# One 512-column product with the weights' hi half for both halves of the operand, in 23 chunks, and the gate bias in two tiles

## The chip, the cores and the metric

The kernel runs on one core of a Trainium2 chip. The metric is the time of one execution on the device in microseconds (us); lower is better. The time before the change is 834.99 us, the median of three runs (832.32 to 836.01).

The core has TensorE (PE; its weight loads are told apart as PEld), VectorE (DVE), ScalarE (ACT) and GpSimd (POOL), which run their own queues in order, and SyncE (SP), whose queue issues the loads from memory here. PE writes to PSUM only, and DVE and ACT take the results from there.

## What is computed

Two blocks of a network over 256 positions of width 1024, in 32-bit floating point. Cut to what the change touches:

```
# first block
h = rmsnorm(x, mix_pre_norm)
u = h @ w_in                       # split into u_z, u_xbc, u_dt, u_ly, u_lx, u_g
y_a = ssd_mixer(u_z, u_xbc, u_dt)  # ends with a norm of y * silu(u_z)
y_b = rglru_mixer(u_ly, u_lx)      # u_lx goes through a causal convolution of 4 taps, two gate products, a scan
g = sigmoid(u_g + gate_b)
x = x + rmsnorm((g0 * (y_a @ w_proj_ssm) + g1 * (y_b @ w_proj_lru)) @ w_out)
x = x + rmsnorm(ffn(rmsnorm(x)))
# second block
cols = rmsnorm(x) @ w_in_2         # split into four branches' inputs (among them xm_q, sw_q, sw_k, sw_v, gm_uv), their z, gate_logits
y_a .. y_m = deltanet, spatial gating, sliding window, memory attention   # each times silu(z)
x = x + rmsnorm(sum_n(sigmoid(gate_logits_n) * (y_n @ w_up_n)) @ w_out_2)
```

## The kernel before

Every weight matrix streams in once, in 129 chunks of two halves (128 x 1024 values each). Of each half ACT makes `whi`, a rounded copy in the fast 32-bit format of PE, and DVE makes `wlo`, the rest (lines 112 and 113). Activations are kept in the same way as `HH` (hi) and `HL` (lo). A product is then three matmuls, hi by hi, hi by lo and lo by hi (`mm3`, lines 425 to 427).

There are two layouts. In `proj_fm` the weights are stationary (128 x 128 blocks) and the activations stream past them, 256 columns (the positions) at a time: one chunk gives 256 output features, in two groups j of 128, each over eight blocks k, so 2 x 8 x 3 = 48 matmuls of 256 columns. In `proj_tm` the activations are stationary and the weights stream, 512 columns at a time, 24 matmuls a chunk.

`Weights` holds three raw halves and five split halves at a time. A load waits until a raw tile is free (its `wlo` done), a split waits until PE has read the tile that it overwrites. All loads stand in SP's queue in order.

PE's order is the order of the code: `Weave` runs the main line (the projections), and at each `yield`, a tick, lets one side line (two in the second block) issue its few instructions. So the matmuls of the recurrent mixers stand between the matmuls of the projections, a fixed number of ticks after what they need was asked for. If that isn't ready, PE waits there. The order on DVE, ACT and SP is set by the framework's scheduler, by when it expects inputs to be ready.

The names that matter below. First block: chunks `ly` (4), `xbc` (6), `z` (4), `lx` (4), `g` (8, layout tm, gate logits, four groups i of two chunks), `pa`, `pb`, `o`. The `z` result is copied from PSUM to `SZ` by one ACT copy of 512 columns a chunk (line 981). The `lx` result goes from PSUM into `conv` (lines 580 to 588: an ACT operation and three DVE operations for each of the two groups, giving `XC`). In the same stretch `side_ssd` runs: for each of 16 heads a PE product `pe`, three ACT exponentials and a DVE product give `M` (line 705), and two ticks later `py` (line 715) reads two `M`. Then `side_lru`: eight products `pg` (line 765) of `XC` with `lw`. The gate bias `gb`, 128 x 2048, is loaded into the buffer of `lw` (lines 990 to 992), so it waits for the last `pg`; DVE adds it to the gate logits of `g` (line 1003). PSUM has four banks (`pp`) for the projections, used in turn.

Second block: `dn` (6 chunks), `xq` (2), `sq` (2), `skv` (1), `gv` (2, tm), `gu` (2), `z2` (8), then `g2` and `up`. Results of `xq`, `sq`, `skv` and `z2` are copied by ACT, 512 columns at a time; `gu` goes through a Gelu from PSUM. They feed the memory branch (`pxs`), the window branch (`psv`, `psc`), and the branches' z.

Of the kernel before, what the change touches and what calls it, by code (L numbers as in the profile page):

```python
# [8 lines left out]
F32 = mybir.dt.float32  # L9
# [187 lines left out]
def two_blocks_kernel(  # L197
# [231 lines left out]
    def proj_fm(name, xh, xl, kouter=False):  # L429
# [19 lines left out]
                    yield  # L449
        return ps, v2(b)  # L450

    def proj_tm(name, xk, nchunk, done, halve=False, before=None):

        w2 = (512, S if halve else 512)
        ps = [[(c0, pbank(f"{name}_{tt}{c0}")) for c0 in range(0, 512, w2[tt])]
              for tt in range(2)]  # L460
        for c in range(nchunk):
            if before:
                yield from before(c)
            wh, wl = W.next(4)
            for tt in range(2):
                t = slice(tt * P, (tt + 1) * P)
                for c0, b in ps[tt]:
                    q = slice(c0, c0 + w2[tt])
                    for k in range(4):
                        h, l = xk(4 * c + k)  # L470
                        mm3(b[:, 0 : w2[tt]], h[:, t], l[:, t], wh[k][:, q], wl[k][:, q],
                            c == 0 and k == 0, c == nchunk - 1 and k == 3)
# [116 lines left out]
                    in1=o[:, d:S], op0=ALU.mult, op1=ALU.add)  # L589


    HH = act8("HH", "HH1", F32R)
    HL = act8("HL", "HL1", F32R)
    wv = Weave(1)

    HU = act8("b3", "HU", F32R)
# [347 lines left out]
            wv.event(f"{nm}{tt}")  # L944
        return then

    def block1(HH, HL):

        late = []
        for p in range(4):  # L950
# [26 lines left out]
            yield  # L977
        SZ = ya["sz"] = act8("b2", "SZ")
        for p in range(4):
            _, b = yield from proj_fm(f"z{p}", HH, HL)  # L980
            nc.scalar.copy(SZ[:, 2 * p : 2 * p + 2, :], b)
            yield
        wv.event("z")
        for p in range(4):
            ps, _ = yield from proj_fm(f"lx{p}", HH, HL)
            two = (2 * p, 2 * p + 1)
            conv([XC[:, i, :] for i in two], ps, "lru_conv_w", two, 8, 4, "lru_conv_b")
            wv.event(f"lx{p}")
            if p == 3:
                gb = big.tile([P, 2 * D], F32, tag="lw", name="gb")  # L990
                with tc.issue_after(W.loaded.ins):
                    nc.sync.dma_start(gb, gbias)
            yield

        G = [big.tile([P, 2, D], F32, tag=("b1", "b9")[n], name=f"G{n}") for n in range(2)]
        for i in range(4):
            n, c = divmod(i, 2)
            q = slice(512 * c, 512 * c + 512)

            def gate(tt, _, ps):  # L1000

                g = G[n][:, tt, q]
                nc.vector.tensor_tensor(out=g, in0=ps, in1=gb[:, 512 * i : 512 * i + 512],  # L1003
                                        op=ALU.add)
                if i == 3:
                    nc.scalar.activation(g, g, AF.Sigmoid)

            yield from proj_tm(f"g{i}", lambda k: (HH[:, k, :], HL[:, k, :]), 2, gate)
            if i == 2:
                nc.scalar.activation(G[0], G[0], AF.Sigmoid)  # L1010
                nc.scalar.activation(G[1][:, :, 0:512], G[1][:, :, 0:512], AF.Sigmoid)
# [23 lines left out]
        yield from M.join(0)  # L1035

        O = []
        HH = act8("HH", "HH2", F32R)
        HL = act8("HL", "HL2", F32R)
        wv.add("n2", side_next("n2", O, HH, HL, "ffn_pre_norm"))  # L1040
        yield from M.out("o", 0, residual("n2", O))

# [26 lines left out]
            yield  # L1069

        O = []
        HH = act8("HH", "HH3", F32R)
        HL = act8("HL", "HL3", F32R)
        wv.add("n3", side_next("n3", O, HH, HL, "norm_pre_2"))
        yield from out_proj("fd", lambda k: (FH[k // 8][:, k % 8, :], FL[k // 8][:, k % 8, :]),
                            6, 1, residual("n3", O), last)
# [2 lines left out]
        yield from proj_tm("mv", lambda k: (em["h"][:, k, :], em["l"][:, k, :]), 2,  # L1079
                           lambda tt, _, ps: nc.scalar.copy(MV[:, tt, :], ps))  # L1080
        yield "n3"
        yield from block2(HH, HL, MK, MV)


    def bc4(ap):
# [4 lines left out]

        return ap.unsqueeze(1).to_broadcast([P, 4, P])

    def block2(HH, HL, MK, MV):
        lws = big.tile([P, 16, P], F32, tag="b8", name="lws")
        wst = lws[:, 0:4, :]
        lvs = lws[:, 4:9, :].rearrange("p a c -> p (a c)")
# [520 lines left out]
                wv.event(f"dn{a}{p}")  # L1617
                yield
        for p in range(2):
            _, b = yield from proj_fm(f"xq{p}", HH, HL)  # L1620
            nc.scalar.copy(XQ[:, 2 * p : 2 * p + 2, :], b)
            if p == 1:
                wv.event("xq")
            yield
        for p in range(2):
            _, b = yield from proj_fm(f"sq{p}", HH, HL)
            nc.scalar.copy(SQ[:, 2 * p : 2 * p + 2, :], b)
            yield
        _, b = yield from proj_fm("skv", HH, HL)
        nc.scalar.copy(SKV, b)  # L1630
        wv.event("skv")
        yield
        yield from proj_tm(
# [1 line left out]
            lambda tt, _, ps: nc.scalar.activation(GV[:, tt, :], ps, AF.Gelu_apprx_tanh))  # L1635
        wv.event("gv")
        for p in range(2):
            _, b = yield from proj_fm(f"gu{p}", HH, HL)
            nc.scalar.activation(GU[:, 2 * p : 2 * p + 2, :], b, AF.Gelu_apprx_tanh)
            if p == 1:  # L1640
                wv.event("gu")
            yield
        for n in (3, 2, 1, 0):
            if n == 0:
                yield "spatial"
            for p in range(2):
                _, b = yield from proj_fm(f"z2{n}{p}", HH, HL)
                nc.scalar.copy(Z[n][:, 2 * p : 2 * p + 2, :], b)
                if p == 1:
                    wv.event(f"z{n}")  # L1650
                yield
# [3 lines left out]
        for n in order:  # L1655
            if n == 0:
                wv.add("y0", branch0())
            G2 = big.tile([P, 2, D], F32, tag="b1", name=f"G2{n}")
            for c in range(2):
                yield from proj_tm(  # L1660
                    f"g2{n}{c}", lambda k: (HH[:, k, :], HL[:, k, :]), 2,
                    lambda tt, _, ps: nc.scalar.activation(
                        G2[:, tt, 512 * c : 512 * c + 512], ps, AF.Sigmoid))
            if n == 3:
                yield "decay"
                yield "delta"
# [12 lines left out]
            if n == order[-1]:  # L1679
                M = Merged(MG, act8("HH", "MH2", F32R), act8("HL", "ML2", F32R), "m2")  # L1680
            for c in range(2):
                q = slice(512 * c, 512 * c + 512)

                def done(tt, _, ps):
                    g, m = G2[:, tt, q], MG[:, tt, q]
                    if n == order[0]:
                        nc.vector.tensor_tensor(out=m, in0=ps, in1=g, op=ALU.mult)
                        return
                    t = tmp(f"mg2{n}{c}{tt}")
                    nc.vector.tensor_tensor(out=t, in0=ps, in1=g, op=ALU.mult)  # L1690
                    nc.vector.tensor_tensor(out=m, in0=m, in1=t, op=ALU.add)
                    if n == order[-1]:
# [19 lines left out]
    def program():  # L1712
        with tc.manual_schedule(engines={nc.scalar.engine, nc.vector.engine}):
            constants()
            for g in range(2):
                for k, _ in enumerate(W.split_pieces(4)):
                    feature(4 * g + k, XT, HU, LU)
                more_loads(g)
            W.split(4)
            for tt in range(2):  # L1720
                nc.scalar.activation(NRM[:, 0:1024], X[:, tt, :], AF.Square,
                                     accum_out=rx[:, tt : tt + 1])
            nc.scalar.activation(rx, rx, AF.Sqrt, bias=eps1, scale=1.0 / D)
            nc.vector.reciprocal(rx, rx)
            dtab.append(small_w(0, 16, "wdt"))
            baab.append(small_w(16, 8, "wba"))
            nc.scalar.activation(ea, row("ssm_a_log"), AF.Exp)
            nc.scalar.activation(ea2, row("a_log_2"), AF.Exp)
            nc.vector.tensor_scalar(nlam, pc[:, lamc : lamc + 8], -1.0, None, op0=ALU.mult)
        yield from block1(HH, HL)  # L1730

    with tc.manual_schedule(engines={nc.tensor.engine}):
        wv.add("rms", side_rms())
# [15 lines left out]
def _layout(inp):  # L1749
# [19 lines left out]
        np.broadcast_to(a(n)[0][None, :], (P, D))  # L1769
        for n in ("mix_post_norm", "ffn_post_norm", "norm_post_2")])  # L1770

    d["gbias"] = np.broadcast_to(a("gate_b")[0].reshape(1, 2 * D), (P, 2 * D))

    parts = []
    for name, n in COLS:
# [94 lines left out]
```

## Time and profile before

| | |
|---|---|
| median of three runs | 834.99 us (832.32 to 836.01) |
| the profiled execution, its own time | 833.6 us |
| its span, first to last instruction | 831.9 us |
| mean granted clock of PE | 0.998 |
| PE busy | 813.5 us, 98% |
| DVE busy | 599.3 us, 72% |
| ACT busy | 519.9 us, 62% |
| POOL busy | 61.1 us, 7% |

The page's times are those of one profiled execution. An operation's duration runs from its start to its end; operations on one engine overlap, so the distance between the starts of two is what one more costs in a row of such. A group's line gives count, busy time and mean duration, then the idle time of the engine just ahead of it and what ended that.

### The profile page before, as it was taken

To read this page: it belongs to the slowest core of one execution; us is meant where nothing else is said; L and a number is where in the kernel's file an instruction comes from. 1 tells how busy PE (TensorE), PEld (TensorE's weight loads), DVE (VectorE), ACT (ScalarE), POOL (GpSimd) and SP (SyncE) were. 2 spreads that over 40 slices of the span, in tenths; PEclk is the share of its full clock that TensorE was granted. 3 is DMA by queue.
4 is the path that set the end of the run, shared out by engine and by line. 5 is a ranking of instruction groups with operands and counts; after the bars stand their busy time and mean duration, and the time that the engine had idled before them with its cause. 6 is when DMAs were issued, how large, how long until landed. Compare 5 with 4: busy or idle time off the path is not lost.

```text
span 831.9 us, 13970 instructions
## 1 busy us (share of the span) xinstructions
PE 813.5 (98%) x5428; PEld 741.5 (89%) x5428; DVE 599.3 (72%) x980; ACT 519.9 (62%) x791; POOL 61.1 (7%) x101
## 2 busy tenths in 40 slices
PE   6999999999999999999999999999999999999997
PEld 6999989778889999999988989998999988888886
DVE  5889678778688788888845597866775547466573
ACT  6575887895656755656644468945966555544452
POOL 0000000000030000000000100028830000000000
PEclk9999999999999999999999999999999999999999
DMA  8546444456754655555655644543554335556551
GB/s 307 194 161 230 142 139 150 169 211 199 250 180 147 218 197 181 176 196 177 209 198 182 196 160 154 199 135 104 164 150 156 121 133 177 194 190 199 190 190 50
DMA packets 41105, 147.15 MB, mean 177 GB/s; under 512 B 4880, under 2 KB 5136, under 8 KB 40784
## 3 DMA queue, kind: packets, MB, share of 16 engines
q1 hardware_dynamic: 40320, 145.35, 51.3%
q0 software_dynamic: 576, 0.92, 0.5%
q8 instruction: 42, 0.69, 0.4%
q14 instruction: 23, 0.19, 0.1%
q10 hardware_dynamic: 144, 0.00, 0.0%
HBM read 144.94 MB, written 1.31 MB: 176 GB/s over the span
## 4 chain that ended last, share of the span: by engine, by line
PE 92%; DVE 4%; DMA 2%; ACT 1%; issue 0%; DVEq 0%; SPq 0%; ACTq 0%
PE fu L427 6%; PE fu L426 6%; PE fu L425 6%; PE g L425 5%; PE g L427 5%; PE g L426 5%; PE z L425 3%; PE z L426 3%; PE z L427 3%; PE fd L426 3%; PE fd L425 3%; PE fd L427 3%; PE up L427 2%; PE up L425 2%; PE up L426 2%; PE o L427 2%
## 5 line engine op out<-in xcount | busy, mean ns | idle before, releaser
L113 DVE TENSOR_TENSOR wlo<-wraw,whi 128x1024 fp32r<-128x1024 f32 x256 | 312.5, 1228 | 145.8 <-ACT whi L112 144.6
L112 ACT CAST whi<-wraw 128x1024 fp32r<-128x1024 f32 x256 | 266.6, 1049 | 219.2 <-PE fu L426 47.5
L425 PE MATMUL fu<-HH,whi 128*128 128x256 f32 x384 | 108.7, 283 | 0.0
L426 PE MATMUL fu<-HL,whi 128*128 128x256 f32 x384 | 108.7, 283 | 0.0
L427 PE MATMUL fu<-HH,wlo 128*128 128x256 f32 x384 | 108.7, 283 | 0.0
L425 PE MATMUL g<-whi,HH 128*128 128x512 f32 x192 | 76.8, 400 | 3.0 <-DVE G L1003 3.0
L427 PE MATMUL g<-whi,HL 128*128 128x512 f32 x192 | 74.9, 390 | 0.0
L426 PE MATMUL g<-wlo,HH 128*128 128x512 f32 x192 | 74.8, 390 | 0.0
L425 PEld LDWEIGHTS fu<-HH,whi 128*128 128x128 f32 x384 | 73.7, 192 | 0.0
L426 PEld LDWEIGHTS fu<-HL,whi 128*128 128x128 f32 x384 | 73.7, 192 | 0.0
L427 PEld LDWEIGHTS fu<-HH,wlo 128*128 128x128 f32 x384 | 73.7, 192 | 0.0
L425 PE MATMUL z<-HH,whi 128*128 128x256 f32 x192 | 56.6, 295 | 0.0
L426 PE MATMUL z<-HL,whi 128*128 128x256 f32 x192 | 54.2, 282 | 0.0
L427 PE MATMUL z<-HH,wlo 128*128 128x256 f32 x192 | 54.2, 282 | 0.0
L425 PEld LDWEIGHTS g<-whi,HH 128*128 128x128 f32 x192 | 36.1, 188 | 10.6 <-DVE G L1003 3.5
L587 DVE SCALAR_TENSOR_TENSOR fc<-fu,pc,fc 128x255 f32<-128x255 f32 (+1 forms) x96 | 43.8, 478 | 1.6
L427 PEld LDWEIGHTS g<-whi,HL 128*128 128x128 f32 x192 | 36.0, 188 | 7.8
L426 PEld LDWEIGHTS g<-wlo,HH 128*128 128x128 f32 x192 | 36.1, 188 | 7.2
L426 PE MATMUL fd<-wlo,FH 128*128 128x512 f32 (+1 forms) x120 | 41.7, 347 | 0.0
L425 PE MATMUL fd<-whi,FH 128*128 128x512 f32 (+1 forms) x120 | 41.6, 347 | 0.0
L427 PE MATMUL fd<-whi,FL 128*128 128x512 f32 (+1 forms) x120 | 41.6, 347 | 0.0
L425 PEld LDWEIGHTS z<-HH,whi 128*128 128x128 f32 x192 | 36.6, 190 | 1.3 <-issue 0.9
(535 smaller groups left out, 2044.1 us busy)
## 6 DMA issues: line engine op xcount, KB each, us to landing
wraw<-in_w_in_dram SPq DMA_DIRECT2D x130, 512.0 KB, 4.0
wraw<-in_w_fu_dram SPq DMA_DIRECT2D x48, 512.0 KB, 4.2
wraw<-in_w_fd_dram SPq DMA_DIRECT2D x24, 512.0 KB, 3.9
wraw<-in_w_o_dram SPq DMA_DIRECT2D x16, 512.0 KB, 4.1
wraw<-in_w_up_dram SPq DMA_DIRECT2D x16, 512.0 KB, 3.6
wraw<-in_w_pa_dram SPq DMA_DIRECT2D x8, 512.0 KB, 3.5
wraw<-in_w_pb_dram SPq DMA_DIRECT2D x8, 512.0 KB, 4.1
wraw<-in_w_mk_dram SPq DMA_DIRECT2D x4, 512.0 KB, 4.2
```

The source lines that it names most:

```text
L112: nc.scalar.copy(hi, raw)
L113: nc.vector.tensor_tensor(out=lo, in0=raw, in1=hi.bitcast(F32), op=ALU.subtract)
L425: nc.tensor.matmul(o, wh, xh, start=first, stop=False)
L426: nc.tensor.matmul(o, wh, xl, start=False, stop=False)
L427: nc.tensor.matmul(o, wl, xh, start=False, stop=last)
L587: nc.vector.scalar_tensor_tensor(o[:, d:S], in0=p[:, 0 : S - d], scalar=col(wname, (taps - 1 - d) * n + i), in1=o[:, d:S], op0=ALU.mult, o ...
```

## The change

In 23 chunks (`z` 4, `lx` 4, `xq` 2, `sq` 2, `skv` 1, `gu` 2, `z2` 8) `proj_fm` gives way to `proj_wide`. HH and HL become one tile `HX`, hi and lo of a block side by side, and `whi` streams both as one product of 512 columns into a whole PSUM bank: hi by hi in columns 0 to 255, hi by lo in 256 to 511. `wlo` by hi goes on top of columns 0 to 255. Each group j has its own bank. Then ACT copies the right half to the result's place and DVE adds the left half to it. For `lx` the result is a new tile `lx_s`, which the convolution reads instead of PSUM; for `gu` the Gelu then runs in place. The other chunks of `proj_fm` and all of `proj_tm` read the same `HX` through views, with the same products as before.

The gate bias is two tiles of 128 x 1024: `gb0` in the buffer `wrow`, which has no earlier user, and `gb1` in that of `lw`.

```
+    def hilo(name):
+        t = big.tile([P, NT, 2, S], F32R, tag="HX", name=name)
+        return t[:, :, 0, :], t[:, :, 1, :], t
...
+    def proj_wide(name, hx, o=None):
+        wh, wl = W.next()
+        ps = [pbank(f"{name}_{j}") for j in range(2)]
+        o = v2(tmp(f"{name}_s")) if o is None else o
+        for j in range(2):
+            f = slice(j * P, (j + 1) * P)
+            for k in range(8):
+                a = (ps[j][:, 0:S], wl[k][:, f], hx[:, k, 0, :])
+                b = (ps[j], wh[k][:, f], hx[:, k].rearrange("p a t -> p (a t)"))
+                for i, p in enumerate((b, a) if k == 0 else (a, b)):
+                    nc.tensor.matmul(*p, start=k + i == 0, stop=k == 7 and i == 1)
+                if k % 4 == 3 and j + k < 8:
+                    yield
+            nc.scalar.copy(o[:, j, :], ps[j][:, S : 2 * S])
+            nc.vector.tensor_tensor(out=o[:, j, :], in0=ps[j][:, 0:S], in1=o[:, j, :], op=ALU.add)
+        return [o[:, j, :] for j in range(2)]
...
-    HH = act8("HH", "HH1", F32R)
-    HL = act8("HL", "HL1", F32R)
+    HH, HL, HX = hilo("HX1")
...
-            _, b = yield from proj_fm(f"z{p}", HH, HL)
-            nc.scalar.copy(SZ[:, 2 * p : 2 * p + 2, :], b)
+            yield from proj_wide(f"z{p}", HX, SZ[:, 2 * p : 2 * p + 2, :])
...
-            ps, _ = yield from proj_fm(f"lx{p}", HH, HL)
+            ps = yield from proj_wide(f"lx{p}", HX)
...
-                gb = big.tile([P, 2 * D], F32, tag="lw", name="gb")
+                gb = [big.tile([P, D], F32, tag=("wrow", "lw")[n], name=f"gb{n}")
+                      for n in range(2)]
                 with tc.issue_after(W.loaded.ins):
-                    nc.sync.dma_start(gb, gbias)
+                    for n in range(2):
+                        nc.sync.dma_start(gb[n], gbias[n])
...
-                nc.vector.tensor_tensor(out=g, in0=ps, in1=gb[:, 512 * i : 512 * i + 512],
-                                        op=ALU.add)
+                nc.vector.tensor_tensor(out=g, in0=ps, in1=gb[n][:, q], op=ALU.add)
...
-        _, b = yield from proj_fm("skv", HH, HL)
-        nc.scalar.copy(SKV, b)
+        yield from proj_wide("skv", HX, SKV)
...
-            _, b = yield from proj_fm(f"gu{p}", HH, HL)
-            nc.scalar.activation(GU[:, 2 * p : 2 * p + 2, :], b, AF.Gelu_apprx_tanh)
+            g = GU[:, 2 * p : 2 * p + 2, :]
+            yield from proj_wide(f"gu{p}", HX, g)
+            nc.scalar.activation(g, g, AF.Gelu_apprx_tanh)
```

What stands where in the queues, at three places. PE, at the start of the chunk `z0`, before:

```order
L425 MATMUL z0_1019<-HH1_103,whi20_832 128x256
L426 MATMUL z0_1019<-HL1_104,whi20_832 128x256
L427 MATMUL z0_1019<-HH1_103,wlo20_833 128x256
L425 MATMUL z0_1019<-HH1_103,whi20_832 128x256
L426 MATMUL z0_1019<-HL1_104,whi20_832 128x256
L427 MATMUL z0_1019<-HH1_103,wlo20_833 128x256
```

and after:

```order
L468 MATMUL z0_0_1018<-HX1_103,whi20_831 128x512
L468 MATMUL z0_0_1018<-HX1_103,wlo20_832 128x256 x2
L468 MATMUL z0_0_1018<-HX1_103,whi20_831 128x512
L468 MATMUL z0_0_1018<-HX1_103,wlo20_832 128x256
L468 MATMUL z0_0_1018<-HX1_103,whi20_831 128x512
```

The first six rows are two blocks k of three products; in the second fence two blocks are the first three rows (four products).

SP's queue, around the load of the gate bias (`wraw` 39 to 49 are raw halves of weights, in the order of use), before:

```order
L87 DMA wraw40_1685<-in_w_in_dram 128x1024
L87 DMA wraw41_1764<-in_w_in_dram 128x1024
L87 DMA wraw42_1770<-in_w_in_dram 128x1024
L87 DMA wraw47_1940<-in_w_in_dram 128x1024
L87 DMA wraw48_1946<-in_w_in_dram 128x1024
L992 DMA gb_1758<-in_gbias_dram 128x2048
L87 DMA wraw49_2024<-in_w_in_dram 128x1024
```

and after:

```order
L87 DMA wraw40_1606<-in_w_in_dram 128x1024
L1015 DMA gb0_1669<-in_gbias_dram 128x1024
L87 DMA wraw41_1677<-in_w_in_dram 128x1024
L87 DMA wraw42_1683<-in_w_in_dram 128x1024
L87 DMA wraw48_1859<-in_w_in_dram 128x1024
L1015 DMA gb1_1670<-in_gbias_dram 128x1024
L87 DMA wraw49_1937<-in_w_in_dram 128x1024
```

The first half of the bias now stands eight weight loads further ahead, between `wraw40` and `wraw41`; the second half stands where the whole stood.

DVE, in the stretch of `lx`, around the product `M13` that `py6` reads (`M13` to `M15` are heads 13 to 15, `lx0_s` is the sum of the chunk `lx0`), before:

```order
L113 TENSOR_TENSOR wlo33_1503<-wraw33_1387,whi33_1502 128x1024
L587 SCALAR_TENSOR_TENSOR XC_123<-lx0_1399,pc_79,XC_123 128x255
L719 SCALAR_TENSOR_TENSOR XS_121<-XS_121,pc_79,py5_1494 128x256
L587 SCALAR_TENSOR_TENSOR XC_123<-lx0_1399,pc_79,XC_123 128x254
L705 TENSOR_TENSOR M13_1489<-M13_1489,bBC_120 128x384
```

and after:

```order
L472 TENSOR_TENSOR lx0_s_1352<-lx0_0_1350,lx0_s_1352 128x256
L727 TENSOR_TENSOR M12_1404<-M12_1404,bBC_119 128x384
L472 TENSOR_TENSOR lx0_s_1352<-lx0_1_1351,lx0_s_1352 128x256
L610 SCALAR_TENSOR_TENSOR XC_122<-lx0_s_1352,pc_79,XC_122 128x255
L741 SCALAR_TENSOR_TENSOR XS_120<-XS_120,pc_79,py5_1435 128x256
L610 SCALAR_TENSOR_TENSOR XC_122<-lx0_s_1352,pc_79,XC_122 128x254
L610 SCALAR_TENSOR_TENSOR XC_122<-lx0_s_1352,pc_79,XC_122 128x255
L610 SCALAR_TENSOR_TENSOR XC_122<-lx0_s_1352,pc_79,XC_122 128x253
L610 SCALAR_TENSOR_TENSOR XC_122<-lx0_s_1352,pc_79,XC_122 128x254
L727 TENSOR_TENSOR M13_1430<-M13_1430,bBC_119 128x384
```

Two additions are new, and `M13` now stands behind five of the six convolution steps of `lx0` instead of two; the split `wlo33` has moved behind it.

## Rows read from the trace of the kernel before

**Rows 1.** The page's first part: busy us (share of the span) x instructions.

```profile
PE 813.5 (98%) x5428; PEld 741.5 (89%) x5428; DVE 599.3 (72%) x980; ACT 519.9 (62%) x791; POOL 61.1 (7%) x101
```

**Rows 2.** The page's chain that ended last: share of the span by engine.

```profile
PE 92%; DVE 4%; DMA 2%; ACT 1%; issue 0%; DVEq 0%; SPq 0%; ACTq 0%
```

**Rows 3.** PE's waits: us in total, times, longest us (the two largest).

```profile
PE ly L425 <- ACT HU L605: 7.0, 1, 7.0
PE g L425 <- DVE G L1003: 3.0, 1, 3.0
```

**Rows 4.** Timeline of PE in a chunk of z: start us, us, instruction.

```profile
83.97 0.28 PE L426 MATMUL z<-HL,whi 128*128 128x256 f32 x1
...
84.69 0.28 PE L426 MATMUL z<-HL,whi 128*128 128x256 f32 x1
```

**Rows 5.** Timeline of PE in a chunk of pa.

```profile
199.74 0.39 PE L426 MATMUL pa<-wlo,YAH 128*128 128x512 f32 x1
199.97 0.39 PE L427 MATMUL pa<-whi,YAL 128*128 128x512 f32 x1
200.19 0.39 PE L425 MATMUL pa<-whi,YAH 128*128 128x512 f32 x1
...
200.65 0.39 PE L427 MATMUL pa<-whi,YAL 128*128 128x512 f32 x1
```

**Rows 6.** Timeline of PE in g, between its groups 1 and 2.

```profile
163.74 0.39 PE L426 MATMUL g<-wlo,HH 128*128 128x512 f32 x1
163.96 0.39 PE L427 MATMUL g<-whi,HL 128*128 128x512 f32 x1
167.38 0.50 PE L425 MATMUL g<-whi,HH 128*128 128x512 f32 x1 [3.03 <-DVE G L1003]
```

**Rows 7.** The chain that ended last, in order of time: start us, us, what.

```profile
160.25 6.36 DMA gb<-in_gbias_dram
166.63 0.70 DVE G L1003
167.38 0.50 PE g L425
```

**Rows 8.** Timeline of DVE, 164.4 to 169.2 us.

```profile
166.63 2.49 DVE L1003 TENSOR_TENSOR G<-g,gb 128x512 f32<-128x512 f32 x4 [0.90 <-DMA gb<-in_gbias_dram]
```

**Rows 9.** Groups of ACT instructions: busy us, mean ns of one.

```profile
L1434 ACT COPY bM<-psv 128x256 f32<-128x256 f32 x1 | 0.4, 373 | 0.5 <-PE psv L1432 0.5
L981 ACT COPY SZ<-z 128x512 f32<-128x512 f32 x4 | 2.4, 590 | 0.6 <-PE z L427 0.6
```

**Rows 10.** Groups of DVE instructions, likewise.

```profile
L1280 DVE TENSOR_TENSOR bLA<-pkk,bLA 128x256 f32<-128x256 f32 x4 | 1.7, 423 | 0.1
```

**Rows 11.** Stretches: length, PE busy (x), PEld, DVE, ACT, POOL, PEclk, DMA share, GB/s.

```profile
73.00:135.00 62.00, 62.00 (x507) 57.78 (x506) 49.50 (x98) 49.12 (x92) 0.31 (x1) 1.00 0.45 152
528.00:663.00 135.00, 135.00 (x1057) 126.23 (x1056) 89.40 (x178) 89.55 (x163) 47.38 (x78) 1.00 0.45 144
```

**Rows 12.** Timeline of DVE, the products M13 and M15.

```profile
115.28 0.55 DVE L705 TENSOR_TENSOR M<-M,bBC 128x384 f32<-128x384 f32 x1
...
118.92 0.55 DVE L705 TENSOR_TENSOR M<-M,bBC 128x384 f32<-128x384 f32 x1
```

**Rows 13.** Timeline of PE, the products py6 and py7.

```profile
117.08 0.44 PE L715 MATMUL py<-M,XD 128*64 128x256 f32 x2
120.94 0.44 PE L715 MATMUL py<-M,XD 128*64 128x256 f32 x2
```

**Rows 14.** Timeline of DVE, two weight splits ahead of pa.

```profile
193.04 2.35 DVE L113 TENSOR_TENSOR wlo<-wraw,whi 128x1024 fp32r<-128x1024 f32 x2
```

**Rows 15.** Timeline of PE, first use of the former of the two.

```profile
196.34 0.39 PE L426 MATMUL pa<-wlo,YAH 128*128 128x512 f32 x1
```

**Rows 16.** Timelines of ACT and PE: the copy of skv, and its transposes.

```profile
571.74 0.57 ACT L1630 COPY bM<-skv 128x512 f32<-128x512 f32 x1
573.39 0.38 PE L1432 MATMUL psv<-ident,bM 128*128 128x128 f32 x2
```

**Rows 17.** Timelines of POOL and PE: the triangular solve's last DMA, and its first reader.

```profile
613.38 2.32 POOL L1219 DMA_DIRECT2D bXY<-dx  x4 [4.66 <-DMA dx<-bM]
635.17 0.56 PE L1301 MATMUL pit<-bXY,bLA 128*128 128x64 f32 x4
```

**Rows 18.** Groups of PE's weight loads (the page's fifth part), `z`.

```profile
L425 PEld LDWEIGHTS z<-HH,whi 128*128 128x128 f32 x192 | 36.6, 190 | 1.3 <-issue 0.9
```

More of the change, by code (lines that the diff above doesn't have):

```diff
@@ L945, in residual, with block1 @@
         return then
-    def block1(HH, HL):
+    def block1(HH, HL, HX):
         late = []
@@ L1037, in block1 @@
         O = []
-        HH = act8("HH", "HH2", F32R)
-        HL = act8("HL", "HL2", F32R)
+        HH, HL, HX = hilo("HX2")
         wv.add("n2", side_next("n2", O, HH, HL, "ffn_pre_norm"))
@@ L1071, in block1 @@
         O = []
-        HH = act8("HH", "HH3", F32R)
-        HL = act8("HL", "HL3", F32R)
+        HH, HL, HX = hilo("HX3")
         wv.add("n3", side_next("n3", O, HH, HL, "norm_pre_2"))
@@ L1081, in block1 @@
         yield "n3"
-        yield from block2(HH, HL, MK, MV)
+        yield from block2(HH, HL, HX, MK, MV)
     def bc4(ap):
@@ L1091, in per4, with block2 @@
         return ap.unsqueeze(1).to_broadcast([P, 4, P])
-    def block2(HH, HL, MK, MV):
+    def block2(HH, HL, HX, MK, MV):
         lws = big.tile([P, 16, P], F32, tag="b8", name="lws")
@@ L1619, in block2 @@
         for p in range(2):
-            _, b = yield from proj_fm(f"xq{p}", HH, HL)
-            nc.scalar.copy(XQ[:, 2 * p : 2 * p + 2, :], b)
+            yield from proj_wide(f"xq{p}", HX, XQ[:, 2 * p : 2 * p + 2, :])
             if p == 1:
@@ L1625, in block2 @@
         for p in range(2):
-            _, b = yield from proj_fm(f"sq{p}", HH, HL)
-            nc.scalar.copy(SQ[:, 2 * p : 2 * p + 2, :], b)
+            yield from proj_wide(f"sq{p}", HX, SQ[:, 2 * p : 2 * p + 2, :])
             yield
-        _, b = yield from proj_fm("skv", HH, HL)
-        nc.scalar.copy(SKV, b)
+        yield from proj_wide("skv", HX, SKV)
         wv.event("skv")
@@ L1646, in block2 @@
             for p in range(2):
-                _, b = yield from proj_fm(f"z2{n}{p}", HH, HL)
-                nc.scalar.copy(Z[n][:, 2 * p : 2 * p + 2, :], b)
+                yield from proj_wide(f"z2{n}{p}", HX, Z[n][:, 2 * p : 2 * p + 2, :])
                 if p == 1:
@@ L1679, in block2 @@
             if n == order[-1]:
-                M = Merged(MG, act8("HH", "MH2", F32R), act8("HL", "ML2", F32R), "m2")
+                M = Merged(MG, *hilo("HXM")[0:2], "m2")
             for c in range(2):
@@ L1729, in program @@
             nc.vector.tensor_scalar(nlam, pc[:, lamc : lamc + 8], -1.0, None, op0=ALU.mult)
-        yield from block1(HH, HL)
+        yield from block1(HH, HL, HX)
     with tc.manual_schedule(engines={nc.tensor.engine}):
@@ L1770, in _layout @@
         for n in ("mix_post_norm", "ffn_post_norm", "norm_post_2")])
-    d["gbias"] = np.broadcast_to(a("gate_b")[0].reshape(1, 2 * D), (P, 2 * D))
+    d["gbias"] = np.broadcast_to(a("gate_b")[0].reshape(2, 1, D), (2, P, D))
     parts = []
```

## The prediction

> **What bounds the kernel now.** I began with the page's first part: PE is busy for 813.5 of 831.9 us [rows 1]. Busy alone proves little, so next the chain that ended last: 92% of it is PE, DVE 4%, DMA 2% [rows 2]. PE is the bound nearly everywhere, and a change counts for what it takes from PE's row of instructions or adds to its waits. PE's waits come third: but for the start (7.0 us for the first activations) one is long, 3.0 us in `g`, behind the DVE addition of the gate bias [rows 3]. Then I measured the step of PE in each layout, from start to start, since a matmul's own duration (0.28 or 0.39 us) overlaps with its neighbours'. In a chunk of `z` six matmuls of 256 columns take 84.69 - 83.97 = 0.72 us, 0.120 each [rows 4]. In `pa` four of 512 columns take 200.65 - 199.74 = 0.91, 0.2275 each [rows 5]. Twice as many columns cost 1.9 times as much.
>
> **The pairs.** A chunk of `proj_fm` has 16 pairs of hi by hi and hi by lo. Each pair goes from two steps of 256 columns, 0.240, to one of 512, 0.2275: 0.0125 us saved. 23 chunks x 16 = 368 pairs, 368 x 0.0125 = 4.6 us, all on PE's own row. The before trace has no stream that alternates 256 and 512 columns, so the size is bounded by single steps of 512 columns: 0.22 (199.97 to 200.19) [rows 5] would give 368 x 0.02 = 7.4 us, and a step of 0.24, just the two old ones, nothing (0.23 is the step of 163.74 to 163.96 in `g` [rows 6]). I take 4.6.
>
> The Trainium skill, "TensorE: Matmul & The Clock Gate", section "Back-to-back issue gap", speaks against this: it gives a warm spacing of N/2.4 + 2.5 ns, by which a pair would save 2.5 ns and the change 0.9 us. The rows are at 120 and 227.5 ns where that formula gives 109 and 216. I go by the rows: a straight line through the two steps has 0.1075 us for 256 columns and 0.0125 that every matmul costs, and one matmul fewer saves that.
>
> **The gate bias.** PE stops after 163.96 + 0.23 = 164.19 and goes on at 167.38 [rows 6]. It needs a PSUM bank that still holds logits, which four DVE additions evacuate from 166.63 on [rows 8]. Those wait for `gb`, issued at 160.25, after the last `pg` has read the buffer, and landing 6.4 us later [rows 7]. With `gb0` in a buffer that nobody used, its load stands eight weight loads earlier, before `wraw41` instead of behind `wraw48`. A chunk takes two halves, so that is four chunks earlier (48 steps of 0.12 each, so over 23 us), and the additions of groups 0 and 1 can follow their products. `gb1` stands where `gb` stood and is needed only when group 2 is done, over 5 us after 167. The 3.0 us go. Late next is the PSUM bank of group 1, evacuated by two DVE operations of 0.7 us, and the weight splits (below). Bounds: 0 to 3.2 us.
>
> **What is added.** Each of 46 groups j gets an ACT copy of 256 columns out of PSUM, 0.373, and a DVE addition of 256 columns with one input in PSUM, 0.423 [rows 9, 10]. The ACT copies of 512 columns (0.590) go in 17 chunks. None of it is on PE. Over `z` and `lx` it is 16 x 0.423 = 6.8 us of DVE on 49.5 in 62, and 16 x 0.373 - 4 x 0.590 = 3.6 of ACT on 49.1 [rows 11]: DVE goes from 80% to some 93% of the (shorter) stretch, ACT to 87%. In the second block 30 x 0.423 = 12.7 us come to 89.4 in 135: 76%. The cover is thin in `z` and `lx` alone. What is queued behind: DVE's in-order queue carries `M` for `py` and the weight splits. I looked at the points where PE would wait.
>
> - `py6`, `py7`. `M13` ends at 115.83 and `py6` starts at 117.08; `M15` ends at 119.47, `py7` starts at 120.94 [rows 12, 13]: 1.25 and 1.5 us to spare. After, DVE has two additions and three more convolution steps ahead of `M13`, but `wlo33` (1.2 us) comes behind it. The two nearly cancel; the ticks are also shorter by 0.05 us. I take 0.4 us of new wait in all (0 to 1.5).
> - The weight splits at `pa`. A `wlo` that ends at 193.04 + 1.2 = 194.25 is read at 196.34 [rows 14, 15]: 2.1 us. PE arrives earlier by 3.0 (the bias) and 8 x 16 x 0.0125 = 1.6, less 0.4: 4.2 us. If the split came no sooner PE would wait 2.1 us. But the four additions (2.49 us) leave the stretch ahead of it [rows 8]. I take 0.7 (0 to 2.1).
> - `skv`. Its ACT copy ends at 572.31 and its transposes start at 573.39 [rows 16]. After, copy, semaphore, addition, and perhaps one split in between: 0.3 us (0 to 1.0).
> - The triangular solve on POOL isn't near: its last DMA is out at 615.7 and first read at 635.17 [rows 17]; ticks that are shorter by some 3 us in all leave that covered.
>
> PSUM: a chunk now takes two banks of four, not one; a bank comes round again after two chunks, over 10 us, and its copy and addition take under 1.
>
> **The sum.** The profiled execution took 833.6 us. 833.6 - 4.6 - 3.0 + 0.4 + 0.7 + 0.3 = 827.4. That execution is 1.4 us under the median of the three runs (834.99), so on the median's scale it would be 828.8; I give the middle, 828.
>
> **The rivals.**
>
> 1. The wait moves instead of going. PE comes 3 us sooner to weight splits that come when they did, since DVE and ACT, not PE, pace the end of block one's recurrence. For: a lead of only 2.1 us [rows 14, 15] and a DVE at 80% before anything is added [rows 11]. Against: four additions leave that stretch. The 3.0 come back, the 0.4 and 0.3 stay: 833.6 - 4.6 + 0.7 = 829.7, 830.4 between the scales. Chance 21%.
> 2. The pair saves nothing: the step of 512 columns next to steps of 256 takes 0.24, since a load of weights takes 0.19 [rows 18] and must fit behind the shorter step. Then 833.6 - 3.0 + 1.4 = 832.0. For: the before trace has no such mixture. Against: both steps have the same fixed part, as a per-matmul cost would, whatever the neighbour. By the page's formula above it would be 831.1. Chance 9%.
> 3. The new additions become the bound (the slower side). Place: DVE from `z` to `pb` and in block two. If every added microsecond of DVE, 46 x 0.423 = 19.5, reached PE as a wait, it would be 833.6 - 7.6 + 19.5 = 845.5. It turns slower by over 0.5% once more than 7.6 + 4.2 = 11.8 us of the 19.5, 60%, come back. For: DVE at 93% in `z` and `lx`. Against: only 6.8 us are in that stretch, and in block two DVE is a third idle [rows 11]. Chance 5%.
> 4. The bias change doesn't do what it says: `gb0` is issued late after all, because SP's queue is in order and the weight loads ahead of it are held by raw buffers. 833.6 - 4.6 + 1.4 = 830.4. Against: it stands eight loads earlier in the queue. Chance 3%.
>
> **How the numbers follow.** The forecast has 62%. About 0.5%, 4.2 us, is what a measurement of this kernel can tell from no change, so faster means under 830.8. That takes nine tenths of the forecast's own spread (0.57), half of rival 1 (0.11) and a little of rival 4: 0.69. Slower takes most of rival 3 and a little beyond: 0.05. The rest, 0.26, is within. For the range: all of the bounds at their best give 833.6 - 7.4 - 3.2 = 823.0, which needs a step of 0.22 throughout; I stop at 824.5. Upward it takes in rivals 1, 4 and 2 on both scales, to 833.5, and leaves out rival 3.
>
> **What would show it.** In the profile after: PE at 5428 - 368 = 5060 instructions; a `z` block k (one of 512, one of 256) stepping at 0.347 us instead of 0.360; no wait of `g` for the bias, and PE's largest wait but the first under 1 us; the additions of groups 0 and 1 between some 140 and 168 us. I am wrong if PE's waits for `wlo` at `pa` or for `py` sum to over 3 us, or if the step of 512 columns in the wide chunks is not 0.2275.

## The result, and the profile after

The changed kernel takes 826.19 us (median of four runs, 825.72 to 826.66) against 835.43 (median of four, 832.32 to 836.01): a ratio of 0.9897, 95% interval 0.9871 to 0.9922. In a second set it was 826.67 against 836.24, 0.9891 (0.9874 to 0.9907). The prediction said 828.0, with a range of 824.5 to 833.5, and faster by over 0.5%. Its sign and its mechanism hold; two of its terms had the wrong size, in opposite directions, and a third came to nothing.

The page's first part, busy time and instructions, and the shares of the chain that ended last (answers to [rows 1, 2]):

```profile
PE 809.6 (98%) x5060; PEld 721.0 (87%) x5060; DVE 612.2 (74%) x1026; ACT 524.6 (64%) x820; POOL 61.0 (7%) x101
...
PE 92%; DVE 5%; ACT 1%; DMA 1%; issue 1%; DVEq 0%; SPq 0%; ACTq 0%
```

PE has 368 instructions fewer and DVE 46 more, as counted. PE is still the whole chain. DVE's busy time grew by 12.9 us, 0.28 for an addition, not 0.42: an operation's duration overlaps with that of its neighbour, so in a row of them it costs less than it lasts. ACT grew by 4.7, not by 46 x 0.373 - 17 x 0.590 = 7.1. The prediction had reckoned with this overlap for PE alone.

PE's waits (answer to [rows 3]; us in total, times, longest):

```profile
PE ly L430 <- ACT HU L627: 7.0, 1, 7.0
PE psst L1256 <- DVE ss L1251: 0.9, 1, 0.9
PE mv L431 <- DVE wlo L113: 0.2, 1, 0.2
PE m1b L943 <- DVE MG L1053: 0.2, 1, 0.2
```

The 3.0 us of `g` are gone, `psst` stood at 0.9 in the page of before too, and there is no wait for `wlo` at `pa`, for `M` at `py`, or for `skv`.

A chunk of `z` on PE (answer to [rows 4]; start us, us, instruction):

```profile
73.01 0.40 PE L468 MATMUL z<-HX,whi 128*128 128x512 f32 x1
73.25 0.28 PE L468 MATMUL z<-HX,wlo 128*128 128x256 f32 x1
73.37 0.40 PE L468 MATMUL z<-HX,whi 128*128 128x512 f32 x1
73.60 0.28 PE L468 MATMUL z<-HX,wlo 128*128 128x256 f32 x1
73.72 0.40 PE L468 MATMUL z<-HX,whi 128*128 128x512 f32 x1
```

Two blocks k take 73.72 - 73.01 = 0.71 us. Over all wide chunks the median step is 233 ns from a product of 512 columns to one of 256, and 117 ns back: 350 for a block k, where the prediction wanted 347.

PE in `g` between its groups 1 and 2 (answer to [rows 6]), then DVE's first four additions of the bias (to [rows 8]), and the two loads of the bias in one row (to [rows 7]; its last two figures are first and last start):

```profile
161.80 0.39 PE L432 MATMUL g<-whi,HX 128*128 128x512 f32 x1
162.02 0.39 PE L430 MATMUL g<-whi,HX 128*128 128x512 f32 x1
162.25 0.39 PE L431 MATMUL g<-wlo,HX 128*128 128x512 f32 x1
```

```profile
144.04 0.69 DVE L1026 TENSOR_TENSOR G<-g,gb 128x512 f32<-128x512 f32 x1 [0.72 <-PE g L432]
147.68 0.69 DVE L1026 TENSOR_TENSOR G<-g,gb 128x512 f32<-128x512 f32 x1 [1.28 <-PE g L432]
160.92 0.68 DVE L1026 TENSOR_TENSOR G<-g,gb 128x512 f32<-128x512 f32 x1
163.44 0.69 DVE L1026 TENSOR_TENSOR G<-g,gb 128x512 f32<-128x512 f32 x1
```

```profile
L1015 SPq DMA_DIRECT2D gb<-in_gbias_dram x2: 328/377/426, 127.1 to 158.1; - x2
```

`gb0` is asked for at 127.1 instead of 160.25 (so rival 4 is out), the additions of groups 0 and 1 stand between 144 and 164 us, wait for PE's products and no longer for a load, and PE goes from group 1 to group 2 in its usual 0.22 us.

The clearest account is by stages. Each figure is the distance between the starts of PE's first product in two chunks, from the timelines:

| us | to `z0` | `z`, `lx` | `g` | `pa` to `mk` | `fu` | `fd` to `dn` | `xq` to the last matmul |
|---|---|---|---|---|---|---|---|
| before, the profile shown | 73.05 | 62.02 | 54.25 | 81.65 | 138.24 | 119.01 | 297.24 |
| after | 71.76 | 61.15 | 50.88 | 81.69 | 138.24 | 118.97 | 295.08 |
| after, a second profile | 71.98 | 61.15 | 50.88 | 81.63 | 138.24 | 118.99 | 295.08 |

The three stages from `pa` to `dn` that the change leaves alone repeat to 0.1 us here (0.3 with the two further profiles of before, below), so differences of that size are readable although whole runs of before spread over 4 us. The stage up to `z0`, which it leaves alone too, does not repeat: it spreads by 1.3. The pairs gave 0.87 + 2.16 = 3.03 us, `g` gave 3.37 (3.2 of it the stop), and 1.29 came before the first wide chunk.

### The profile page after: what moved, and what is told of

Same layout as the page of the kernel before. It is cut to its first block, busy times and chain, and to the rows that moved or that the text cites. A ratio compares the mean times of both kernels' runs of the same rounds, so it can differ in the third digit from the quotient of the medians.

```text
span 824.0 us, 13302 instructions
## 1 busy us (share of the span) xinstructions
PE 809.6 (98%) x5060; PEld 721.0 (87%) x5060; DVE 612.2 (74%) x1026; ACT 524.6 (64%) x820; POOL 61.0 (7%) x101
## 4 chain that ended last, share of the span: by engine, by line
PE 92%; DVE 5%; ACT 1%; DMA 1%; issue 1%; DVEq 0%; SPq 0%; ACTq 0%
PE z L468 8%; PE fu L432 6%; PE fu L431 6%; PE fu L430 6%; PE g L430 5%; PE g L432 5%; PE g L431 5%; PE lx L468 3%; PE fd L431 3%; PE fd L432 3%; PE fd L430 3%; PE up L430 2%; PE up L431 2%; PE up L432 2%; PE o L432 2%; PE o L430 2%
## 5 line engine op out<-in xcount | busy, mean ns | idle before, releaser
L430 PE MATMUL fu<-HX,whi 128*128 128x256 f32 x384 | 108.7, 283 | 0.0
L431 PE MATMUL fu<-HX,whi 128*128 128x256 f32 x384 | 108.7, 283 | 0.0
L432 PE MATMUL fu<-HX,wlo 128*128 128x256 f32 x384 | 108.7, 283 | 0.0
L430 PE MATMUL g<-whi,HX 128*128 128x512 f32 x192 | 76.7, 399 | 0.0
L432 PE MATMUL g<-whi,HX 128*128 128x512 f32 x192 | 74.9, 390 | 0.0
L431 PE MATMUL g<-wlo,HX 128*128 128x512 f32 x192 | 74.8, 390 | 0.0
L430 PEld LDWEIGHTS fu<-HX,whi 128*128 128x128 f32 x384 | 73.7, 192 | 0.0
L431 PEld LDWEIGHTS fu<-HX,whi 128*128 128x128 f32 x384 | 73.7, 192 | 0.0
L432 PEld LDWEIGHTS fu<-HX,wlo 128*128 128x128 f32 x384 | 73.7, 192 | 0.0
L468 PE MATMUL z<-HX,whi 128*128 128x512 f32 x192 | 70.1, 402 | 0.0
L468 PE MATMUL z<-HX,wlo 128*128 128x256 f32 x192 | 51.0, 286 | 0.0
L432 PEld LDWEIGHTS g<-whi,HX 128*128 128x128 f32 x192 | 36.0, 188 | 7.7
L430 PEld LDWEIGHTS g<-whi,HX 128*128 128x128 f32 x192 | 36.1, 188 | 7.2
L468 PEld LDWEIGHTS z<-HX,wlo 128*128 128x128 f32 x192 | 36.2, 189 | 1.5
```

Of the source, the lines that this page charges most:

```text
L430: nc.tensor.matmul(o, wh, xh, start=first, stop=False)
L431: nc.tensor.matmul(o, wh, xl, start=False, stop=False)
L432: nc.tensor.matmul(o, wl, xh, start=False, stop=last)
L468: nc.tensor.matmul(*p, start=k + i == 0, stop=k == 7 and i == 1)
```

## The experiments

### Two more profiles of the kernel before

No edit.

> The kernel before once more, unaltered, for a second profile of it. Its median is 835.4 to 836.2 us, but its one profiled execution took 833.6. The kernel with the wide products alone stopped in g for 3.4 us, and PE's granted clock stood at 0.50 for about 6 us behind that stop: 2.8 us more than the stop itself. Theory: in most executions of before the stop in g is a little longer than the 3.03 us of its first profile and the clock falls behind it too: an execution over 835 us shows steps of 0.43 us in the chunk of g behind the stop, and 2 to 3 us lost there. Rival: the spread lies in the waits of the first ten chunks, and the clock stays at 1.00 in g.

> The same kernel again, for a third profile, as one execution may be of either kind. The same theory and rival: over 835 us with the clock at 0.50 behind the stop in g, under 834 us with it at 1.00.

They took 834.76 and 834.50 us. By stages: 72.00 and 71.74 to `z0`, 62.02 in `z` and `lx`, 56.45 and 56.18 in `g`, 297.24 from `xq` on. So the 1.29 us at the start were chance (0.24 and -0.02 are left of them), and `g` takes 2 us more than in the first profile. PE in `g`, in the first of the two:

```profile
162.91 0.39 PE L427 MATMUL g<-whi,HL 128*128 128x512 f32 x1
167.00 0.79 PE L425 MATMUL g<-whi,HH 128*128 128x512 f32 x1 [3.69 <-DVE G L1003]
167.59 0.63 PE L426 MATMUL g<-wlo,HH 128*128 128x512 f32 x1
168.01 0.63 PE L427 MATMUL g<-whi,HL 128*128 128x512 f32 x1
168.44 0.63 PE L425 MATMUL g<-whi,HH 128*128 128x512 f32 x1
```

And three stretches of it (columns as in [rows 11]; the granted clock is the 1.00 or 0.50 ahead of the DMA share):

```profile
162.00:167.00 5.00, 1.30 (x7) 0.76 (x5) 3.44 (x6) 4.97 (x5) 0.00 (x0) 1.00 0.97 342
167.00:170.00 3.00, 3.00 (x7) 2.42 (x8) 3.00 (x5) 2.97 (x4) 0.00 (x0) 0.50 0.99 382
171.00:174.00 3.00, 3.00 (x15) 2.47 (x14) 0.01 (x1) 1.49 (x2) 0.00 (x0) 1.00 0.52 161
```

Behind the stop PE steps at 0.43 us for 512 columns instead of 0.227, with the clock at 0.50, that is 1.2 GHz instead of 2.4, until about 170.2. PE is reckoned as busy all that time, and neither the waits nor the chain name the loss. In the second of the two PE comes back at 2.4 GHz and the clock falls 1.3 us later, for as long (steps of 0.43 us from 168.07 on):

```profile
166.43 0.50 PE L425 MATMUL g<-whi,HH 128*128 128x512 f32 x1 [3.39 <-DVE G L1003]
167.46 0.39 PE L426 MATMUL g<-wlo,HH 128*128 128x512 f32 x1
167.69 0.58 PE L427 MATMUL g<-whi,HL 128*128 128x512 f32 x1
168.07 0.63 PE L425 MATMUL g<-whi,HH 128*128 128x512 f32 x1
```

The first profile of before, with a stop of 3.03, shows 1.00 throughout; the other two, with 3.69 and 3.39, show the slow stretch. The theory holds but for its bounds: the chunk behind the stop takes 7.15 and 7.19 us instead of 5.44 (after), so 1.7 are lost, and executions of 834.5 to 834.8 have it already. The Trainium skill, "TensorE: Matmul & The Clock Gate", section "HAM oscillation — how this bites in real kernels", tells of such a return at half clock after PE waited for a transfer. The first of these two profiles agrees (granted clock 0.50 from 167.0 us on), the second only from 1.3 us after the return on, and the profile with the stop of 3.03 doesn't show it.

### The bias alone

The kernel before, with the edit of `gb` and its addition as in the change's diff, and nothing else.

> The kernel before with the gate bias alone in two tiles; all chunks as before. Theory: the 3.0 us stop in g goes and nothing takes its place: 3.0 to 3.4 us under before (about 831.8 on a median of 835.0), no wait of PE over 1 us behind the first. Rival (the wait moves): PE reaches the weight splits at pa 3 us sooner and waits there for 1 to 3 us; under 2 us gained.

829.84 us against 836.24, ratio 0.9928 (0.9912 to 0.9944): 6.4 us, twice the theory. In its profile `g` takes 50.88, as after, and no clock falls; the rest is that of before, but for 0.6 us that come back between `pa` and `mk` (0.3 in the second chunk of `pa`, the rest at `m1b`) and 0.5 at `psst` in `dn`. Rival 1 of the prediction, 3 us moved on to the weight splits, is out but for those 0.3. In `g` the part is worth 3.4 to 5.6 us, by the profile of before that it is set against.

### The wide products alone

The changed kernel with `gb` as before:

```
-                gb = [big.tile([P, D], F32, tag=("wrow", "lw")[n], name=f"gb{n}")
-                      for n in range(2)]
+                gb = big.tile([P, 2 * D], F32, tag="lw", name="gb")
```

> The changed kernel with the gate bias in one tile again, in the buffer of lw, so with the wide products alone. Theory: 368 pairs x 8 ns = 3.0 us under before, and 3.0 to 3.4 us over the changed kernel, about 829.4; PE stops in g for 3 to 4 us behind the bias again (it comes there a little sooner). If a pair saved 12.5 ns, it would be 4.6 us under before. If the two parts help each other (a queue shared with the new additions), the sum of the two single gains differs from the whole by over 1 us.

831.44 against 836.24, ratio 0.9949 (0.9934 to 0.9965). `z` and `lx` take 61.15 and the stretch from `xq` on 295.08, exactly as after: the pairs give their 3.03 us without the bias part. The stop is 3.4 us in its profile, as the theory said, and then:

```profile
165.94 0.79 PE L430 MATMUL g<-whi,HX 128*128 128x512 f32 x1 [3.44 <-DVE G L1024]
166.53 0.63 PE L431 MATMUL g<-wlo,HX 128*128 128x512 f32 x1
```

```profile
166.00:172.00 6.00, 6.00 (x14) 4.72 (x15) 3.94 (x5) 4.64 (x4) 0.00 (x0) 0.50 0.77 289
```

PE ran 14 products in 6 us at half clock. `g` took 57.42, 6.5 more than without the stop: 3.6 for the stop and 2.9 in the chunk behind it. This execution took 832.79, the longest of its six (831.03 to 832.79): how much is lost behind the stop changes from run to run. The two single gains, 6.4 and 4.8, don't add up to the whole, 9.6. The mean granted clock, which is known of every execution, also where no trace was kept, points to why. It is 0.998 or 0.999 in all executions of the changed kernel and of the bias alone. In the 11 of before in this set it is 0.994 to 0.996 with a median of 0.994, and in the six of the wide products alone 0.994 to 0.999 with a median of 0.996. A difference of 0.002 is some 1.7 us of 835 (an estimate from these clocks, which are rounded to 0.001), and the sum of the gains is 1.6 over the whole. So by the clocks the stop cost more in before than with the wide products alone, and that the parts help each other isn't needed to explain it.

### The bias in pieces

The kernel before, one tile, four loads:

```
-                    nc.sync.dma_start(gb, gbias)
+                    for n in range(4):
+                        nc.sync.dma_start(gb[:, 512 * n : 512 * n + 512],
+                                          gbias[:, 512 * n : 512 * n + 512])
```

> The kernel before with the gate bias still in one tile in the buffer of lw, but loaded by four transfers of 512 columns, so that the additions of the first group wait for a quarter alone. All chunks as before. Theory (a stop of 3 us costs its own length and mostly the clock behind it): the stop becomes 0.3 to 1.5 us, the clock stays at 1.00, and the time comes to within 1 us of the kernel with the bias in two tiles (829.8), 830 to 831. Rival (what counts is the place in the queue): all four transfers land as late as the one, and the time stays at 835 to 836.

830.91 against 836.35, ratio 0.9932 (0.9919 to 0.9946).

```profile
162.89 0.39 PE L427 MATMUL g<-whi,HL 128*128 128x512 f32 x1
164.34 0.50 PE L425 MATMUL g<-whi,HH 128*128 128x512 f32 x1 [1.07 <-DVE G L1005]
164.68 0.39 PE L426 MATMUL g<-wlo,HH 128*128 128x512 f32 x1
```

A stop of 1.07 us, steps back near 0.23 at once, a granted clock of 0.999 in all five executions, and a time 1.1 us over that of the kernel with two tiles: this short stop costs little more than its length (`g` takes 1.4 us longer than there). The first load stands where the one load stood, the other three one weight load later, and the stop is short all the same, so the rival is out. Shortening the stop by 2 to 2.6 us brought 5.4.

### Another order in the wide chunks

```
+            for h in range(2):
+                a = [(ps[j][:, 0:S], wl[k][:, f], hx[:, k, 0, :])
+                     for k in range(4 * h, 4 * h + 4)]
+                b = [(ps[j], wh[k][:, f], hx[:, k].rearrange("p a t -> p (a t)"))
+                     for k in range(4 * h, 4 * h + 4)]
+                for i, p in enumerate(b + a if h == 0 else a + b):
```

> The changed kernel with another order inside the wide chunks: in each half of the weights the four products of 512 columns stand in a row, then the four of 256, and in the next half the four of 256 first. The same products and the same sum but for its order. Theory (the neighbour sets the step: 233 and 117 ns alternating, 227 and 120 ns among their own kind): the pair of 512 and 256 goes from 350 to 347 ns, 368 x 3 = 1.1 us less than the changed kernel, about 825.1. Rival (350 ns is the sum whatever the order, set by the weight loads): no difference, 826.2. Second rival: runs of 256 columns let the 190 ns weight loads show, over 120 ns: slower than the changed kernel.

826.20 against 836.24, ratio 0.9883 (0.9867 to 0.9900): the changed kernel's time (0.9891). By stages `z` and `lx` and the stretch from `xq` on gain 0.26 us together, not 1.1, and in this profile `pa` to `mk` takes 0.65 more than after. The theory falls in this form. A row of products of 512 columns starts with steps of 234, 233, 230, 232, 231 ns (medians by place in the row) and only from the sixth on has 227; a row of 256 starts with 117, 118, 119 and has 120 from the fourth on. With rows of four and eight PE hardly reaches the level that I had taken from pure streams.

### Which operand makes the step

```
+                if name[0:2] == "z2":
+                    a = (ps[j], wl[k][:, f], b[2])
+                elif name[0] == "z":
+                    b = (ps[j], wh[k][:, f], h[:, 512 * (k % 2) : 512 * (k % 2) + 512])
+                elif name[0:2] == "lx":
+                    b = (ps[j], hx[:, k, 0, f], b[2])
+                elif name[1] == "q":
+                    a = (ps[j][:, S : 2 * S], wl[k][:, f], hx[:, k, 0, :])
```

> The changed kernel with other operands in some wide chunks, to see what makes a block k step at 350 ns instead of the 347 (227 + 120) that the two layouts had shown; its results are other ones there. In z the product of 512 columns streams the weights' own hi half instead of HX; in lx its stationary operand is a block of HX instead of the weights; in xq and sq the product of 256 columns goes to the right half of the bank; in z2 the product with the weights' lo half streams 512 columns too; skv and gu are as in the changed kernel. Theory A (the streamed tile makes it): z at 347, the others at 350. Theory B (the stationary tile): lx at 347. Theory C (that both products add into the same columns): xq, sq at 347. Theory D (256 beside 512, whatever the order): z2 at 2 x 227 = 454, none of the others at 347; if z2 steps at 2 x 232 = 464, D is wrong.

One run, 842.65 us. In `z`, `lx`, `xq` and `sq` a block k steps within 2 ns of what it takes there in the changed kernel (medians of 347 to 354 in both; `xq` is at 347 in both): theories A to C are out. The edit's condition also takes in the third of the four `z` chunks, which is named `z2` as well, so only three show theory A. In the eight chunks `z2` of the second block, with 512 columns throughout:

```profile
598.02 0.39 PE L478 MATMUL z<-HX,whi 128*128 128x512 f32 x1
598.24 0.39 PE L478 MATMUL z<-HX,wlo 128*128 128x512 f32 x1
598.47 0.39 PE L478 MATMUL z<-HX,whi 128*128 128x512 f32 x1
598.70 0.39 PE L478 MATMUL z<-HX,wlo 128*128 128x512 f32 x1
598.92 0.39 PE L478 MATMUL z<-HX,whi 128*128 128x512 f32 x1
```

0.90 us for four, and a median of 227 each over all eight chunks: D holds. It is the mixture of lengths within a few products, not the streamed tile, the stationary one or the columns written, that costs some 3 ns a pair.

### The additions doubled

```
+            nc.scalar.copy(o[:, j, :], ps[j][:, S : 2 * S])
+            nc.vector.tensor_tensor(out=o[:, j, :], in0=ps[j][:, 0:S], in1=o[:, j, :], op=ALU.add)
             nc.scalar.copy(o[:, j, :], ps[j][:, S : 2 * S])
             nc.vector.tensor_tensor(out=o[:, j, :], in0=ps[j][:, 0:S], in1=o[:, j, :], op=ALU.add)
```

> The changed kernel with ACT's copy and DVE's addition of each of the 46 groups done twice over, one behind the other, to the same result: DVE gets another 46 x 0.42 = 19.4 us, ACT another 46 x 0.375 = 17.3 us, of work that nothing needs, and each result comes 0.8 us later. Theory: the additions are hidden behind PE with room to spare but in z and lx, where DVE is at 83% already: 826.5 to 829, with waits of PE for wlo at pa (0.6 us to spare now) and py of 0 to 2 us. Rival (the additions are at the edge of being the bound): over 832.

828.23 against 836.35, ratio 0.9904 (0.9890 to 0.9918): 1.6 us more than the changed kernel, in its profile 1.33 in `z` and `lx` and 0.91 from `xq` on. Rival 3 of the prediction is out: the cover holds for a second set of additions nearly whole. It is thin just where the prediction looked. In `lx`, the chain in order of time:

```profile
113.45 0.33 DVE lx_s L472
113.79 0.41 DVE XC L612
...
114.95 0.47 DVE XC L612
115.42 0.48 DVE M L729
115.91 0.04 issue
115.95 0.86 PE py L739 x5
```

`M13` stands behind additions and convolution steps in DVE's queue, and `py6` waits for it. The other place is `skv`:

```profile
PE psv L1454 <- DVE bM L474: 0.7, 1, 0.7
```

### Wide products in `xbc` and `dn`

```
-            ps, _ = yield from proj_fm(f"xbc{p}", HH, HL)
+            ps = yield from proj_wide(f"xbc{p}", HX)
...
+                    ps = yield from proj_wide(f"dn{a}{p}", HX)
```

> The changed kernel with the wide product also in xbc (6 chunks) and in dn but its first (5 chunks), whose convolutions then read the sum instead of PSUM, as in lx. 11 x 16 = 176 more pairs of 8 ns: 1.4 us under the changed kernel, 825.2, if the additions are hidden (DVE is at 85% in xbc and 83% in dn before them, and gets 22 x 0.42 = 9.3 us). Rival (additions stand ahead of the next weight split or delay the results): waits of PE for wlo or pcb, pxt, delta of 1 to 4 us in all, 826.7 to 829.

827.54 against 835.34, ratio 0.9910 (0.9897 to 0.9924): no gain over the changed kernel (0.9891), as the rival had it. Up to `z0` its profile is ahead by 1.3 us, of which six chunks of pairs at 8 ns are 0.8 and chance may be the rest. Then PE waits 0.3 for a `wlo` and loses 0.7 in all over `z` and `lx`; from `xq` on it loses 0.8, most of it (0.6) at a side line's transposes at once behind `dn`; and in `dn` such transposes wait longer for their input from DVE (0.9 after):

```profile
516.73 0.44 PE L1256 MATMUL psst<-ident,ss 128*128 128x128 f32 x2 [2.04 <-DVE ss L1251]
```

### Wide products in `fu`

```
-                ps, _ = yield from proj_fm(f"fu{a}_{p}", HH, HL, p + a == 0)
+                if a + p == 0:
+                    ps, _ = yield from proj_fm(f"fu{a}_{p}", HH, HL, True)
+                else:
+                    ps = yield from proj_wide(f"fu{a}_{p}", HX)
```

> The changed kernel with the wide product also in fu but its first chunk (23 chunks, 46 groups). 368 more pairs of 8 ns: 3.0 us under the changed kernel, 823.7, if hidden. Against it: DVE is at 82% there (4.75 us in a chunk of 5.76) and gets 2 x 0.42 a chunk: 5.6 us in a chunk that would take 5.63. Rival (here the additions do become the bound): DVE over 97% in fu, PE waits for wlo in fu, a chunk as long as before or longer, 826.7 to 835.

822.23 us against 835.34, ratio 0.9841 (0.9828 to 0.9855): the fastest version, some 4 us under the changed kernel (3.84 in the stage of `fu`). The stretch of `fu`, after and here:

```profile
271.20:403.70 132.50, 132.50 (x1106) 132.50 (x1105) 109.58 (x161) 80.79 (x117) 0.00 (x0) 1.00 0.56 190
```

```profile
271.20:399.80 128.60, 128.60 (x738) 112.03 (x737) 120.57 (x206) 96.26 (x162) 0.00 (x0) 1.00 0.58 194
```

PE never waits; a chunk takes 5.593 us instead of 5.760. DVE is at 94%, not 99%, for the reason told above: 46 additions of 0.42 raised its busy time by 12.0 over the whole execution (624.2 against 612.2), 0.26 each. No side line stands in `fu`, so each result has a whole chunk of time. Here a pair saves 0.167 / 16 = 10.4 ns, just 360 less 350.

## Why the prediction was right, and which terms were wrong

**The pairs: right in kind, too large.** Predicted 4.6, measured 3.03, 8.2 ns a pair. The step that failed is the straight line through two pure streams: 0.2275 for a product of 512 columns and 0.120 for one of 256 are not what either takes in a mixture, and the sign that I had set for being wrong (a step of 512 other than 0.2275) is there. A block k of 350 instead of 347 explains 2.1 of the 4.3 ns that are missing: in `fu`, where no side line stands between, a pair saves 10.4. The other 2.2 are missing only where side lines' matmuls stand between (6.8 ns a pair saved in `z` and `lx`, 9.0 from `xq` on). The timelines of `z` and `lx` show where they went. The side lines' own matmuls take 14.5 us before and after, and both have 16 steps that are some 0.1 us longer than the others; without those, a block k took 358 ns on average before, not 360, and 351 after. So the lengths were mixed before too, by the side lines, and the trace of before already held steps under 0.120. No run takes the side lines away, so that they are the cause is inferred. Rival 2, no gain, is out. By the formula for single matmuls in the Trainium skill, "TensorE: Matmul & The Clock Gate", section "Back-to-back issue gap", a block k is estimated at 325 ns after and 328 before; the rows of `fu` have 350 and 360, so a matmul less saves four times as much as by it.

**The gate bias: right, too small.** Predicted 3.0, at most 3.2; 3.4 to 5.6 by the profiles and 6.4 by the times. The step read the wait from one profile, took it as the whole price, and so, without naming it, took the clock of that profile (1.00) for that of all executions. In the other two the clock is at 0.50 for a while behind the stop.

**The new waits: sized at 1.4, measured at 0.** The margins were foreseen in the right places and shrank without closing in both profiles of the changed kernel. DVE's `M13` and PE's `py6` (answers to [rows 12, 13]):

```profile
113.94 0.56 DVE L727 TENSOR_TENSOR M<-M,bBC 128x384 f32<-128x384 f32 x1
```

```profile
115.26 0.87 PE L737 MATMUL py<-M,XD 128*64 128x256 f32 x8
```

0.76 us to spare instead of 1.25. At `pa` the first of three splits and its first use (to [rows 14, 15]; the first split ends about 190.4):

```profile
189.23 3.49 DVE L113 TENSOR_TENSOR wlo<-wraw,whi 128x1024 fp32r<-128x1024 f32 x3
```

```profile
190.81 0.39 PE L431 MATMUL pa<-wlo,YAH 128*128 128x512 f32 x1
```

0.4 us instead of 2.1: PE comes 5.5 us earlier, the split 3.8. Of both, 1.3 is the earlier start; the rest, 4.2 and 2.5, is what the prediction had for PE and for the four additions that leave the stretch, so its own figures left 0.4 to spare, and the 0.7 that it took was caution. But the additions alone don't bring 2.5: with the bias alone the split comes 1.2 us earlier beyond the start, PE 3.4, and that is the wait of 0.3 us in `pa`. What brings the other 1.3 isn't shown. At `skv` the addition ends at 565.82 and the transposes start at 567.04, with a split ahead of the addition, as foreseen (to [rows 16]):

```profile
565.41 0.41 DVE L472 TENSOR_TENSOR bM<-skv,bM 128x256 f32<-128x256 f32 x1
```

**That the sum came out near is luck in part.** From its own starting point, the profile of 833.6, the two measured parts give 833.6 - 3.03 - 3.37 = 827.2 where the prediction had 827.4: the pairs 1.6 too large, the bias 0.4 too small and the waits 1.4 too large cancel. On the scale of the medians the smaller gain of the pairs is made up for by what a stop costs behind it, which no term held.

**DVE in `z` and `lx`** was put at 93%; it is 85%, with nine operations more in the stretch, not 16, that cost less than they last (answer to [rows 11]):

```profile
72.00:133.00 61.00, 61.00 (x378) 50.88 (x377) 51.99 (x107) 50.14 (x99) 0.31 (x1) 1.00 0.45 153
```

**What the profiles of before leave out.** Three profiled executions of before took 833.6 to 834.8, the medians of its runs 835.3 to 836.4. The stages account for 8.8 us between its second profile and that of after; 0.8 of the 9.6 in the second set lie outside them. The granted clocks point to where. The three profiles have 0.998 (no slow stretch), 0.996 and 0.996 (over 3 us at half clock), and the profile of the wide products alone has 0.994 (nearly 7 us). In the second set (836.24) and the third (836.35) 14 of the 20 executions of before are at 0.994 or 0.995, with medians of 836.4 and 837.0 us, and six at 0.996 or 0.997, with 835.0 and 835.2; in the fourth set (835.34) two of nine are at 0.994 (836.3 and 836.7), and the rest at 0.996. So by their clocks many executions ran longer at half clock than any kept profile of before shows. What stays open is how long the stop itself was in them, and what makes it and the loss vary.

## What to carry to other kernels

A stop of TensorE can cost more than its length: look at the granted clock and at the steps behind it, in more than one profile, before pricing its removal. Fewer, longer matmuls saved only 7 to 10 ns each here, and least among side work, but many of them in a stretch that is bound by PE and free of side work add up (23 chunks of `fu`, 4 us). DVE's spare time in such a stretch matters less than what stands in its queue ahead of the operation that PE waits for.

## What the runs showed of the hardware that was not expected

- After stops of 3.4 to 3.7 us PE ran at 1.2 GHz (granted clock 0.50) for 3 to 7 us, in one profile only from 1.3 us after its return on; after stops of 3.03 and 1.07 us it kept 2.4 GHz.
- The step of a 512-column product depends on the last few products, not on its neighbour alone: 233 ns amid 256 columns, 227 from the sixth in a row of its own length.
- An addition of 256 columns lasts 0.42 us and adds 0.26 to 0.33 us to DVE's busy time (12.9 us for 46 in the change, 12.0 for 46 in `fu`, 15.0 for 46 when doubled).
